# The first values of an attention layer: the two halves of the sum taken in turn over four token tiles, in four PSUM banks, with the loads in that order

## The chip, the cores and the metric

The kernel runs on one core of one Trainium2 chip. Its time is the device time in microseconds of one execution; a lower time is better. The core has five engines that run side by side, each with its own in-order queue: PE (matrix products; its weight loads, PEld, lie beside its products), DVE (vector), ACT (scalar, one function per element), POOL (general) and SP, which only issues DMAs here. DMAs are carried out by 16 DMA engines that the queues share.

## The reference, cut to what matters

The reference is a trunk of two layers: an attention layer and a recurrent layer, each followed by a SwiGLU feed-forward network, on one sequence of 1024 tokens of width 1024 in float32. The change touches only the start of the attention layer.

```
def reference(x, attn_w_in, ...):
    for layer in range(DEPTH):
        h = rmsnorm(x, norm_mix_pre[layer])
        if layer % 2 == 0:
            m = attention_mixer(h, attn_w_in[j], attn_rel_bias[j], attn_w_out[j])
...

def attention_mixer(h, w_in, rel_bias, w_out):
    proj = h @ w_in
    part_a, part_b = proj[..., :3 * A_W], proj[..., 3 * A_W:]
    qa, ka, va = [...]
    qs, ks, vs = [...]
    out_a = chunked_relpos_attention(qa, ka, va, rel_bias)
    out_b = stick_breaking_attention(qs, ks, vs)
    return jnp.concatenate([out_a, out_b], axis=-1) @ w_out
```

There are 16 heads of width 64. The values v of four heads are 256 columns of `h @ w_in`: for each token a sum over 1024 input columns.

## The kernel before, in words

**Tiles.** A token tile is 128 tokens (t = 0 to 7). The inner dimension, 1024, is cut into eight kt of 128. Each float32 operand is held as a high and a low part in the matmul's faster float32 type, and a product is three matmuls: high by high, high by low, low by high (lines 291 to 293 for the values, 166 to 168 for queries and keys). `split` (lines 140 to 159) makes the two parts of a weight tile: a cast on ACT (L155), then the rest on DVE (L156).

**The start.** The input comes in twice. `x_t` is the input with the inner dimension on the partitions: four column groups c of 256 tokens (two token tiles), each in two halves q of four kt; one load is 512 KB (`load_cols`, L464). `take(c)` multiplies these by the norm's gain `g0` and splits them into `hT`: on ACT (L495) and then DVE (L496), four kt for each of the two halves. `x` itself comes in rows, a token tile per load of 512 KB (`load_rows`, L459); it serves only the norm's scale: `squares(t)` sums the squares of a row on ACT (L501), and POOL (L503, L504) makes the reciprocal root `rsc` of it. The value weights of four heads come as two halves of the inner dimension (`w_v[grp, 0]` and `w_v[grp, 1]`, L137, 512 KB each), matching q.

**The values.** `v_tile(grp, w, vt, t2)` makes the unscaled values of the token tiles 2·t2 and 2·t2 + 1 in one PSUM bank, 256 columns each: 2 x 8 x 3 = 48 matmuls of 256 columns, the first token tile over all eight kt, then the second. Four calls, 192 matmuls, make the first group. `evacuate(vt, t2)` empties the bank: ACT multiplies with `rsc` while it copies (L305 and L306, 128 columns each, two token tiles). The banks come from a pool `proj` with two buffers, and the first projection of queries (L166 to L168, `psq`) takes its banks from the same pool: its first half of the tokens can start when token tiles 4 and 5 have been emptied, its second half when 6 and 7 have. `spread(half)` turns four `rsc` into a row `rsb` with DVE (L511), PE (a pair of matmuls, L513) and a copy by ACT (L514).

**The order.** The kernel's text gives the priorities: weights half 0, `take(0)`, weights half 1, `v_tile` 0, `take(1)`, `v_tile` 1, the squares of rows 0 and 1, `evacuate` 0, `take(2)`, `v_tile` 2 and so on. The framework then lays out each engine's own order from a simulated timeline (line 1257), so that an instruction whose inputs come late by that timeline is overtaken by others of its engine. SP issues the loads in this order: `g0`, weights half 0, columns (0,0) and (0,1), weights half 1, columns (1,0), (1,1), (2,0), (2,1), rows 0 and 1, columns (3,0), (3,1), rows 2 and 3; then the query and key weights and rows 4 to 7 in between. Ahead of the first product PE runs 32 transposes of an identity (L483), which read no input.

**Scores.** Behind the first projection the attention's scores take banks of a third PSUM pool, `pp`, tag `sc`, three buffers (L399, L400).

Of the kernel before, what the change touches and what calls it, by code (L numbers as in the profile page):

```python
# [8 lines left out]
F32 = mybir.dt.float32  # L9
F32R = mybir.dt.float32r  # L10
BF16 = mybir.dt.bfloat16
AF = mybir.ActivationFunctionType
ALU = mybir.AluOpType
PSUM = bass.MemoryType.PSUM

P = 128
S = 1024
D = 1024
KT = D // P
# [80 lines left out]
class Trunk:  # L100
# [164 lines left out]
    def attention(self, x_src, xT_src, w_v, w_qk, bias_t, o_dst, hT, pools, open_first):  # L265
        nc, tc = self.nc, self.tc
        with ExitStack() as ctx:
            ap = ctx.enter_context(tc.tile_pool(name="att", bufs=1, reuse_waits="tile"))
            pp = ctx.enter_context(tc.tile_pool(name="attp", bufs=1, space=PSUM, side="right", reuse_waits="tile"))
            prj = ExitStack()  # L270
            prp = prj.enter_context(tc.tile_pool(name="attproj", bufs=1, space=PSUM, reuse_waits="tile"))
# [6 lines left out]
            def v_weights(grp):  # L278
                return [self.split(w_v[grp, j], 4, 256) for j in range(2)]

            def v_tile(grp, w, vt, t2):
                ps = prp.tile([P, 512], F32, tag="proj", bufs=2, name=self.uid("psv"))
                for tt in range(2):
                    t = 2 * t2 + tt
                    hh, hl = hT.half[t // 4]
                    tok = slice((t % 4) * P, (t % 4) * P + P)
                    o = ps[:, tt * 256:(tt + 1) * 256]
                    for kt in range(KT):
                        wh, wl = w[kt // 4]
                        k4 = kt % 4  # L290
                        nc.tensor.matmul(o, hh[:, kt, tok], wh[:, k4, :], start=kt == 0, stop=False)
                        nc.tensor.matmul(o, hh[:, kt, tok], wl[:, k4, :], start=False, stop=False)
                        nc.tensor.matmul(o, hl[:, kt, tok], wh[:, k4, :], start=False, stop=kt == KT - 1)
                psvs[t2] = ps.rearrange("p (a h b) -> p a h b", a=2, h=2)

            psvs = {}

            def evacuate(vt, t2, both=False):
                psv = psvs.pop(t2)
                for tt in range(2):  # L300
                    t = 2 * t2 + tt
                    if both:
                        nc.vector.tensor_scalar(vt[0][:, t, :], psv[:, tt, 0, :], rsc[:, t:t + 1], None, op0=ALU.mult)
                    else:
                        nc.scalar.activation(vt[0][:, t, :], psv[:, tt, 0, :], AF.Copy, scale=rsc[:, t:t + 1])  # L305
                    nc.scalar.activation(vt[1][:, t, :], psv[:, tt, 1, :], AF.Copy, scale=rsc[:, t:t + 1])  # L306

            def steps(vt):
                for v in vt:
# [8 lines left out]
            def v_alloc():  # L318
                return [ap.tile([P, NT, P], F32, tag="v", bufs=3, name=self.uid("v")) for _ in range(2)]
# [133 lines left out]
            vt = v_alloc()  # L453
            small = ap.tile([P, 64], F32, name="small")
            ssc, rsc, g0 = small[:, 0:NT], small[:, 8:8 + NT], small[:, 16:16 + KT]

            def load_rows(t):
                x = ap.tile([P, D], F32, tag="st", bufs=12, name=self.uid("x0"))
                self.last_load = nc.sync.dma_start(x, x_src[t * P:(t + 1) * P, :]).ins  # L459
                return x  # L460

            def load_cols(c, q):
                x = ap.tile([P, D], F32, tag="st", bufs=12, name=self.uid("xt")).rearrange("p (k t) -> p k t", k=4)
                nc.sync.dma_start(x, xT_src[c, q])  # L464
                return x

            nc.sync.dma_start(g0, self.io["g0col"])
            grp = seq[0] // 2
            cols, rows_in = {}, {}
            raws = [self.raw(w_v[grp, 0], 4)]  # L470
            cols[0] = [load_cols(0, 0), load_cols(0, 1)]
            raws.append(self.raw(w_v[grp, 1], 4))
            for c in range(1, 4):
                cols[c] = [load_cols(c, 0), load_cols(c, 1)]
                if c > 1:
                    for t in (2 * c - 4, 2 * c - 3):
                        rows_in[t] = load_rows(t)

            ones = ap.tile([P, 640], F32, tag="nata", bufs=3, name=self.uid("ones"))[:, 0:P]
            nc.vector.memset(ones, 1.0)  # L480
# [2 lines left out]
                nc.tensor.transpose(warm[:, 0:P], self.ident, self.ident)  # L483
            rsb = ap.tile([P, S], F32, name="rsb")

            def take(c):
                hh, hl = hT.half[c // 2]
                ts = slice((c % 2) * 256, (c % 2) * 256 + 256)
                for q in range(2):
                    x = cols[c][q]  # L490
                    for k in range(4):
                        kt = 4 * q + k
                        g = g0[:, kt:kt + 1]
                        hi = hh[:, kt, ts]
                        nc.scalar.activation(hi, x[:, k], AF.Copy, scale=g)  # L495
                        nc.vector.scalar_tensor_tensor(hl[:, kt, ts], x[:, k], g, hi.bitcast(F32),  # L496
                                                       op0=ALU.mult, op1=ALU.subtract)

            def squares(t):
                x = rows_in[t]  # L500
                nc.scalar.activation(x, x, AF.Square, scale=D ** -0.5, accum_out=ssc[:, t:t + 1])  # L501
                r = rsc[:, t:t + 1]
                nc.gpsimd.tensor_scalar(r, ssc[:, t:t + 1], EPS, None, op0=ALU.add)  # L503
                nc.gpsimd.tensor_tensor(r, r, self.neghalf, op=ALU.pow)  # L504
# [8 lines left out]
                nc.tensor.matmul(ps, ones, d, start=True, stop=True)  # L513
                nc.scalar.copy(rsb[:, half * HALF:(half + 1) * HALF], ps)  # L514

            w0 = self.split(None, 4, 256, raw=raws[0])
            take(0)
            wv = [w0, self.split(None, 4, 256, raw=raws[1])]
            v_tile(grp, wv, vt, 0)
            take(1)  # L520
            v_tile(grp, wv, vt, 1)
            squares(0); squares(1)
            evacuate(vt, 0)
            take(2)
            v_tile(grp, wv, vt, 2)
            squares(2); squares(3)
            evacuate(vt, 1)
            take(3)
            v_tile(grp, wv, vt, 3)
# [8 lines left out]
            wq = self.split(None, KT, P, raw=wq)  # L538
            squares(4); squares(5)
            evacuate(vt, 2)  # L540
            squares(6); squares(7)
            evacuate(vt, 3)
# [4 lines left out]
            for j, p in enumerate(seq):  # L547
# [4 lines left out]
                if j < 7:  # L552
                    q = seq[j + 1]
                    if q % 2 == 0:
                        wv = v_weights(q // 2)
                        vt = v_alloc()
# [704 lines left out]
```

## Time and profile before

| What | us |
|---|---|
| Median of 3 runs | 2187.07 |
| The runs | 2186.4, 2187.07, 2189.74 |
| The profiled execution | 2190.47 |
| its span, first to last instruction | 2188.7 |
| PE's first product of the values (L291) | at 6.95 |
| PE's first projection product (L166) | at 35.62 |

The profile is of one execution. In its views a line of a timeline has the start, the duration, the engine, the line of the kernel, the operation, the tile written and the tiles read, and, where the engine stood idle ahead of it, for how long and what ended the idle time. The granted clock of PE is given as a share of full speed. A matmul's duration in the trace is longer than the distance to the next one, since matmuls overlap; what a matmul costs PE is that distance.

### The profile page before, as it was taken

To read this page: it belongs to the slowest core of one execution; us is meant where nothing else is said; L and a number is where in the kernel's file an instruction comes from. 1 tells how busy PE (TensorE), PEld (TensorE's weight loads), DVE (VectorE), ACT (ScalarE), POOL (GpSimd) and SP (SyncE) were. 2 spreads that over 40 slices of the span, in tenths; PEclk is the share of its full clock that TensorE was granted. 3 is DMA by queue.
4 is the path that set the end of the run, shared out by engine and by line. 5 is a ranking of instruction groups with operands and counts; after the bars stand their busy time and mean duration, and the time that the engine had idled before them with its cause. 6 is when DMAs were issued, how large, how long until landed. Compare 5 with 4: busy or idle time off the path is not lost.

```text
span 2188.7 us, 30464 instructions
## 1 busy us (share of the span) xinstructions
PE 2160.6 (99%) x11140; PEld 1803.1 (82%) x11140; DVE 1502.0 (69%) x2458; ACT 1171.6 (54%) x2174; POOL 210.3 (10%) x398
## 2 busy tenths in 40 slices
PE   9999999999999999999999999999999999999998
PEld 8898989878788888888887777888788888888886
DVE  4747555556877677767768678437786767758675
ACT  6656555556855545433446676538755454424453
POOL 2111113121100000000002333102100000000011
PEclk9999999999999999999999999999999999999999
DMA  7111011126334233336468411356233333328565
GB/s 284 44 40 59 30 38 56 45 93 216 135 98 138 92 121 96 112 100 242 135 194 241 128 57 39 110 189 228 76 131 101 122 96 102 106 87 292 169 182 155
DMA packets 169039, 272.32 MB, mean 124 GB/s; under 512 B 14140, under 2 KB 95036, under 8 KB 168888
## 3 DMA queue, kind: packets, MB, share of 16 engines
q1 hardware_dynamic: 168248, 268.27, 38.3%
q10 hardware_dynamic: 640, 2.10, 0.3%
q8 instruction: 87, 1.43, 0.3%
q14 instruction: 64, 0.52, 0.1%
HBM read 202.69 MB, written 65.54 MB: 123 GB/s over the span
## 4 chain that ended last, share of the span: by engine, by line
PE 88%; DVE 4%; DMA 3%; ACT 2%; issue 2%; POOL 0%; SPq 0%; POOLq 0%; ACTq 0%; DVEq 0%
PE ps L752 13%; PE ps L753 13%; PE ps L751 13%; PE ps L594 7%; PE ps L837 5%; PE ps L838 5%; PE ps L836 5%; PE pso L366 3%; PE tr L431 3%; PE psq L166 3%; PE psq L167 2%; PE psq L168 2%; PE ps L166 2%; PE ps L167 2%; PE ps L168 2%
## 5 line engine op out<-in xcount | busy, mean ns | idle before, releaser
L752 PE MATMUL ps<-hS,q 128*128 128x512 f32 (+1 forms) x1288 | 489.8, 380 | 0.5 <-DVE hS L89 0.5
L751 PE MATMUL ps<-hS,q 128*128 128x512 f32 (+1 forms) x1288 | 490.0, 381 | 0.0
L753 PE MATMUL ps<-hS,q 128*128 128x512 f32 (+1 forms) x1288 | 489.3, 380 | 0.0
L722 DVE TENSOR_TENSOR q<-raw,q 128x512 fp32r<-128x512 f32 x308 | 205.6, 687 | 175.1 <-ACT q L721 174.3
L752 PEld LDWEIGHTS ps<-hS,q 128*128 128x128 f32 x1288 | 242.9, 189 | 47.1 <-DVE hS L89 0.9
L751 PEld LDWEIGHTS ps<-hS,q 128*128 128x128 f32 x1288 | 242.5, 189 | 46.4 <-DVE tf L89 0.5
L753 PEld LDWEIGHTS ps<-hS,q 128*128 128x128 f32 x1288 | 243.0, 189 | 45.6
L721 ACT CAST q<-raw 128x512 fp32r<-128x512 f32 x308 | 178.7, 616 | 172.5 <-DVE raw L730 116.9
L837 PE MATMUL ps<-o,o 128*128 128x512 f32 x616 | 240.2, 390 | 0.6 <-DVE o L832 0.6
L838 PE MATMUL ps<-o,o 128*128 128x512 f32 x616 | 237.9, 390 | 0.3 <-DVE o L966 0.3
L836 PE MATMUL ps<-o,o 128*128 128x512 f32 x616 | 221.6, 391 | 3.5 <-ACT o L965 3.0
L709 ACT ACTIVATE raw<-raw,gcol 128x256 f32<-128x256 f32 x352 | 150.4, 498 | 131.2 <-DMA raw<-in_ffn_w_up_dram 73.2
L831 ACT CAST o<-raw 128x512 fp32r<-128x512 f32 x184 | 110.3, 620 | 161.7 <-PE ps L838 49.4
L182 POOL TENSOR_SCALAR rs<-ss 128x1 f32<-128x1 f32 x52 | 25.2, 484 | 1420.3 <-ACT junk L178 1355.8
L832 DVE TENSOR_TENSOR o<-raw,o 128x512 fp32r<-128x512 f32 x184 | 123.5, 689 | 54.4 <-ACT o L831 53.7
L836 PEld LDWEIGHTS ps<-o,o 128*128 128x128 f32 x616 | 115.4, 188 | 30.5 <-ACT o L965 5.1
L837 PEld LDWEIGHTS ps<-o,o 128*128 128x128 f32 x616 | 115.7, 188 | 25.8 <-DVE o L832 2.1
L838 PEld LDWEIGHTS ps<-o,o 128*128 128x128 f32 x616 | 115.6, 188 | 24.8 <-DVE o L966 1.2
L156 DVE TENSOR_TENSOR wlo<-raw,whi 128x1024 fp32r<-128x1024 f32 x76 | 93.6, 1231 | 57.4 <-ACT whi L155 56.3
L419 DVE TENSOR_TENSOR_SCAN pr<-pr,zero 128x128 f32<-128x128 f32 (+7 forms) x64 | 86.6, 1358 | 51.3 <-POOL pr L416 49.6
L155 ACT CAST whi<-raw 128x1024 fp32r<-128x1024 f32 x76 | 79.7, 1049 | 48.5 <-PE ps L167 19.9
L166 PE MATMUL psq<-hT,whi 128*128 128x512 f32 x256 | 102.3, 400 | 0.2 <-DVE st L337 0.2
(206 smaller groups left out, 4263.8 us busy)
## 6 DMA issues: line engine op xcount, KB each, us to landing
raw<-in_ffn_w_gate_dram SPq DMA_DIRECT2D x44, 512.0 KB, 4.2
raw<-in_ffn_w_up_dram SPq DMA_DIRECT2D x44, 512.0 KB, 4.2
gS<-c SPq DMA_DIRECT2D x88, 256.0 KB, 3.7
raw<-gS SPq DMA_DIRECT2D x88, 256.0 KB, 2.9
gA<-c SPq DMA_DIRECT2D x66, 256.0 KB, 3.3
raw<-in_ffn_w_down_dram SPq DMA_DIRECT2D x63, 256.0 KB, 4.4
raw<-gA SPq DMA_DIRECT2D x44, 256.0 KB, 2.8
t<-in_ffn_w_down_dram SPq DMA_DIRECT2D x22, 512.0 KB, 6.6
```

The source lines that it names most:

```text
L166: nc.tensor.matmul(ps, wh[:, kt, cols], hh[:, kt, :], start=kt == 0, stop=False)
L594: self.matmul = nc.tensor.matmul(ps[:, n * 512:(n + 1) * 512], x, y[:, n, :], start=first and i == 0, stop=last and i == len(passes) - 1).ins
L709: nc.scalar.activation(raw[:, i], raw[:, i], AF.Copy, scale=gain[:, 4 * k + i:4 * k + i + 1])
L721: self.last = nc.scalar.copy(t[:, 0], src).ins
L722: self.last_lo = nc.vector.tensor_tensor(t[:, 1], src, t[:, 0].bitcast(F32), op=ALU.subtract).ins
L751: nc.tensor.matmul(ps, a[:, 0, kt, :], bh, start=kt == 0, stop=False)
L752: nc.tensor.matmul(ps, a[:, 0, kt, :], bl, start=False, stop=False)
L753: self.matmul = nc.tensor.matmul(ps, a[:, 1, kt, :], bh, start=False, stop=kt == 3).ins
L832: tt(t[:, 1], src, t[:, 0].bitcast(F32), op=ALU.subtract)
L836: nc.tensor.matmul(ps, a[0], b[:, 0], start=first, stop=False)
L837: nc.tensor.matmul(ps, a[0], b[:, 1], start=False, stop=False)
L838: nc.tensor.matmul(ps, a[1], b[:, 0], start=False, stop=last)
```

## The change

The first four token tiles of the first value group are made together. For each half q of the inner dimension the weights' half is split, then for c = 0 and 1 the columns of (c, q) are taken and the twelve matmuls of this half are issued for the two token tiles of c. The four sums stay open meanwhile, in four banks: token tiles 0 and 2 in the two banks of `proj`, 1 and 3 in two of the three banks of `sc`. Token tiles 4 to 7 are made as before. `evacuate` and its dictionary go by token tile in place of pairs. The loads are put in the order of use: weights half 0, columns (0,0), (1,0), weights half 1, columns (0,1), (1,1), then rows 0 and 1, columns (2,0), (2,1), rows 2 and 3, columns (3,0), (3,1). The load of `g0` is issued by ACT in place of SP.

```diff
+            def v_part(o, w, t, kts):
+                hh, hl = hT.half[t // 4]
+                tok = slice((t % 4) * P, (t % 4) * P + P)
+                psvs[t] = o.rearrange("p (h b) -> p h b", h=2)
+                for kt in kts:
+                    wh, wl = w[kt // 4]
+                    k4 = kt % 4
+                    nc.tensor.matmul(o, hh[:, kt, tok], wh[:, k4, :], start=kt == 0, stop=False)
+                    nc.tensor.matmul(o, hh[:, kt, tok], wl[:, k4, :], start=False, stop=False)
+                    nc.tensor.matmul(o, hl[:, kt, tok], wh[:, k4, :], start=False, stop=kt == KT - 1)
+
+            def v_bank():
+                return prp.tile([P, 512], F32, tag="proj", bufs=2, name=self.uid("psv"))
+
             def v_tile(grp, w, vt, t2):
-                ps = prp.tile([P, 512], F32, tag="proj", bufs=2, name=self.uid("psv"))
+                ps = v_bank()
                 for tt in range(2):
...
+                    v_part(ps[:, tt * 256:(tt + 1) * 256], w, 2 * t2 + tt, range(KT))
...
-            nc.sync.dma_start(g0, self.io["g0col"])
+            nc.scalar.dma_start(g0, self.io["g0col"])
             grp = seq[0] // 2
-            cols, rows_in = {}, {}
-            raws = [self.raw(w_v[grp, 0], 4)]
-            cols[0] = [load_cols(0, 0), load_cols(0, 1)]
-            raws.append(self.raw(w_v[grp, 1], 4))
-            for c in range(1, 4):
-                cols[c] = [load_cols(c, 0), load_cols(c, 1)]
-                if c > 1:
-                    for t in (2 * c - 4, 2 * c - 3):
-                        rows_in[t] = load_rows(t)
+            cols, rows_in, raws = {}, {}, []
+            for q in range(2):
+                raws.append(self.raw(w_v[grp, q], 4))
+                for c in range(2):
+                    cols[c, q] = load_cols(c, q)
+            for c in range(2, 4):
+                for t in (2 * c - 4, 2 * c - 3):
+                    rows_in[t] = load_rows(t)
+                for q in range(2):
+                    cols[c, q] = load_cols(c, q)
...
-            def take(c):
+            def take(c, qs=(0, 1)):
...
-            w0 = self.split(None, 4, 256, raw=raws[0])
-            take(0)
-            wv = [w0, self.split(None, 4, 256, raw=raws[1])]
-            v_tile(grp, wv, vt, 0)
-            take(1)
-            v_tile(grp, wv, vt, 1)
+            wv = []
+            banks = [(pp.tile([P, 512], F32, tag="sc", bufs=3, name=self.uid("psv")) if t % 2 else v_bank())[:, 0:256]
+                     for t in range(4)]
+            for q in range(2):
+                wv.append(self.split(None, 4, 256, raw=raws[q]))
+                for c in range(2):
+                    take(c, (q,))
+                    for tt in range(2):
+                        v_part(banks[2 * c + tt], wv, 2 * c + tt, range(4 * q, 4 * q + 4))
             squares(0); squares(1)
             evacuate(vt, 0)
```

More of the change, by code (lines that the diff above doesn't have):

```diff
@@ L281, in v_tile @@
+            def v_bank():
+                return prp.tile([P, 512], F32, tag="proj", bufs=2, name=self.uid("psv"))
             def v_tile(grp, w, vt, t2):
-                ps = prp.tile([P, 512], F32, tag="proj", bufs=2, name=self.uid("psv"))
+                ps = v_bank()
                 for tt in range(2):
[L284 to L293, printed above, removed]
@@ L294, in v_tile @@
-                psvs[t2] = ps.rearrange("p (a h b) -> p a h b", a=2, h=2)
+                    v_part(ps[:, tt * 256:(tt + 1) * 256], w, 2 * t2 + tt, range(KT))
             psvs = {}
             def evacuate(vt, t2, both=False):
-                psv = psvs.pop(t2)
-                for tt in range(2):
-                    t = 2 * t2 + tt
+                for t in (2 * t2, 2 * t2 + 1):
+                    psv = psvs.pop(t)
                     if both:
-                        nc.vector.tensor_scalar(vt[0][:, t, :], psv[:, tt, 0, :], rsc[:, t:t + 1], None, op0=ALU.mult)
+                        nc.vector.tensor_scalar(vt[0][:, t, :], psv[:, 0, :], rsc[:, t:t + 1], None, op0=ALU.mult)
@@ L304, in evacuate @@
                     else:
-                        nc.scalar.activation(vt[0][:, t, :], psv[:, tt, 0, :], AF.Copy, scale=rsc[:, t:t + 1])
-                    nc.scalar.activation(vt[1][:, t, :], psv[:, tt, 1, :], AF.Copy, scale=rsc[:, t:t + 1])
+                        nc.scalar.activation(vt[0][:, t, :], psv[:, 0, :], AF.Copy, scale=rsc[:, t:t + 1])
+                    nc.scalar.activation(vt[1][:, t, :], psv[:, 1, :], AF.Copy, scale=rsc[:, t:t + 1])
             def steps(vt):
@@ L484, in attention @@
             rsb = ap.tile([P, S], F32, name="rsb")
-            def take(c):
+            def take(c, qs=(0, 1)):
                 hh, hl = hT.half[c // 2]
                 ts = slice((c % 2) * 256, (c % 2) * 256 + 256)
-                for q in range(2):
-                    x = cols[c][q]
+                for q in qs:
+                    x = cols[c, q]
                     for k in range(4):
```

## The prediction

> **What bounds the kernel now.** I read the page's shares first, then busy time by stretch for the start, then the timelines of PE and ACT there.
>
> ```profile
> span 2188.7 us, 30464 instructions
> PE 2160.6 (99%) x11140; PEld 1803.1 (82%) x11140; DVE 1502.0 (69%) x2458; ACT 1171.6 (54%) x2174; POOL 210.3 (10%) x398
> ```
>
> PE has 28 us of idle time in the span. Whatever the change wins must come out of the first 58 us; behind them PE has hardly any idle time for a long way (x counts instructions; of each engine the busy time in the stretch; then granted clock, DMA share, GB/s):
>
> ```profile
> core 0: us, PE busy (x) PEld busy (x) DVE busy (x) ACT busy (x) POOL busy (x), PEclk, DMA share, GB/s
> 6.90:9.37 2.47, 2.39 (x13) 1.75 (x12) 2.47 (x7) 2.47 (x7) 0.00 (x0) 1.00 1.04 421
> 9.37:11.94 2.57, 0.89 (x3) 0.48 (x3) 2.42 (x5) 2.57 (x6) 0.00 (x0) 1.00 1.02 406
> 11.94:15.56 3.62, 3.62 (x17) 3.62 (x18) 3.62 (x10) 3.62 (x10) 0.00 (x0) 0.53 1.03 412
> 15.56:29.01 13.45, 13.45 (x114) 13.45 (x113) 8.21 (x20) 13.45 (x32) 3.56 (x10) 1.00 1.03 404
> 4.90:29.40 24.50, 22.74 (x162) 21.33 (x161) 17.50 (x39) 24.05 (x54) 3.95 (x10) 0.93 1.03 409
> 58.00:440.00 382.00, 381.32 (x2874) 337.62 (x2873) 232.85 (x428) 221.68 (x449) 60.85 (x122) 1.00 0.14 46
> ```
>
> The reader is to see three limits that lie close together. PE loses 9.37 to 11.94 nearly whole, then runs 3.6 us at half clock. ACT is busy 24.05 of 24.50 us. The DMA engines are full, at 409 GB/s, so a load of 512 KB lands every 524288 B / 409 GB/s = 1.28 us, whatever the order. PE's timeline has the edges:
>
> ```profile
> 6.95 0.39 PE L291 MATMUL psv<-whi,hT 128*128 128x256 f32 x1
> 10.68 0.80 PE L291 MATMUL psv<-whi,hT 128*128 128x256 f32 x2 [1.31 <-ACT whi L155]
> 11.94 0.43 PE L292 MATMUL psv<-wlo,hT 128*128 128x256 f32 x1 [0.34 <-DVE wlo L156]
> 29.01 1.02 PE L513 MATMUL tr<-diag,ones 128*128 128x512 f32 x2
> 29.99 0.28 PE L292 MATMUL psv<-wlo,hT 128*128 128x256 f32 x1
> 35.62 0.40 PE L166 MATMUL psq<-hT,whi 128*128 128x512 f32 x1
> 41.09 1.02 PE L513 MATMUL tr<-diag,ones 128*128 128x512 f32 x2
> ```
>
> The values' 192 matmuls run from 6.95 to 35.62, and both waits are for the second weight tile. The clock by stretches of 3.41 us, laid on the grid on which it changes:
>
> ```profile
> 8.73:12.14 3.41, 1.72 (x9) 1.12 (x9) 3.26 (x7) 3.41 (x8) 0.00 (x0) 1.00 1.02 408
> 12.14:15.55 3.41, 3.41 (x17) 3.41 (x17) 3.41 (x10) 3.41 (x10) 0.00 (x0) 0.50 1.03 413
> 445.64:449.05 3.41, 1.72 (x12) 1.44 (x12) 3.29 (x14) 2.80 (x6) 0.67 (x1) 1.00 1.03 405
> 1199.94:1203.36 3.42, 2.06 (x10) 1.41 (x9) 3.42 (x5) 1.10 (x2) 0.00 (x0) 1.00 0.45 108
> 1203.36:1206.77 3.41, 3.41 (x16) 2.79 (x16) 2.28 (x3) 1.15 (x2) 1.60 (x2) 1.00 0.89 271
> 449.05:452.46 3.41, 3.41 (x12) 2.72 (x12) 1.88 (x9) 2.19 (x8) 2.03 (x4) 0.50 0.61 224
> 1548.10:1551.50 3.40, 3.40 (x19) 3.40 (x18) 2.14 (x4) 3.22 (x8) 0.79 (x2) 0.51 0.41 167
> ```
>
> A stretch with 3.41 - 1.72 = 1.69 us of idle PE is followed by one at 0.50; one with 3.42 - 2.06 = 1.36 us is not. A halved stretch full of matmuls costs 3.41 / 2 = 1.7 us, and this execution has three. The Trainium skill ("TensorE: Matmul & The Clock Gate", section "Why this matters for your kernels") asks for no PE idle gaps over about 3 us. This trace is stricter, at 1.69 us; by the page the half clock at 12.14 would not have come from the wait, and 1.7 us less would be to be had in the profiled execution.
>
> **The change part by part.** *The small load goes to ACT's queue.* SP's first weight load moves up by one issue:
>
> ```profile
> 0.72 0.40 SPq L467 DMA_DIRECT2D small<-in_g0col_dram  x1
> 1.18 0.42 SPq L137 DMA_DIRECT2D raw<-in_attn_w_v_dram  x1
> 2161.47 0.50 ACTq L258 DMA_DIRECT2D out_dram<-x  x1
> ```
>
> That is 1.18 - 0.72 = 0.46 us for every landing while the DMA engines are full. On ACT the issue costs about 0.50, before the first weights have landed, so it hides. If the DMA engines start no earlier, the 0.46 is lost; if ACT's issue delayed its first cast, up to 0.50 more. I take 0.46.
>
> *The order of the sum.* Its first half needs weight half 0 and two column loads (launch positions 1 to 3); the second half needs positions 4 to 6. A block of four kt and two token tiles holds PE for 24 x 13.45 / 114 = 2.83 us, and ACT makes the operands of two such blocks in this time:
>
> ```profile
> 5.04 1.05 ACT L155 CAST whi<-raw 128x1024 fp32r<-128x1024 f32 x1 [3.03 <-DMA raw<-in_attn_w_v_dram]
> 6.39 3.30 ACT L495 ACTIVATE hT<-xt,small 128x256 fp32r<-128x256 f32 x8 [0.30 <-DMA xt<-in_x_t_dram]
> ```
>
> that is 3.30 / 2 = 1.65 us for one. So PE has 5.7 us of work while ACT makes the next block (1.65) and casts the second weights (1.05): the wait at 9.37 goes, and with it the half clock behind it. PE alone then takes: start 6.95 - 0.46 = 6.49; the first 12 matmuls as now, still paced by the split, about 2.3 us (first stretch above); 180 x 0.118 = 21.2; the pair on L513 with what it displaces, 29.99 - 29.01 - 0.12 = 0.86. Sum 30.8 against 35.62: 4.8 us early. The later column loads stand behind row loads now, two positions (2.6 us) later for c=2 and c=3. c=3's second half moves from position 12 to 14, landing at about 5.0 + 13 x 1.28 - 0.46 = 21.2 us (the first weights' cast starts at 5.04); PE wants it behind 6.5 of 8 parts of its 192 matmuls, at about 26, and ACT needs 1.65 us. If ACT did the squares of four rows first, PE could wait about 1 us there. I take 0.
>
> *What is late next: a PSUM bank.* The first projection (L166) writes the bank of token tiles 4 and 5, which ACT has to empty first (L305, L306), with a scale from the square of row 5 (L501). ACT's timeline there:
>
> ```profile
> 28.34 1.05 ACT L155 CAST whi<-raw 128x1024 fp32r<-128x1024 f32 x1
> 30.07 0.59 ACT L514 COPY rsb<-tr 128x512 f32<-128x512 f32 x1 [0.68 <-PE tr L513]
> 31.07 1.07 ACT L501 ACTIVATE x<-x 128x1024 f32<-128x1024 f32 x1
> 33.48 0.36 ACT L306 ACTIVATE v<-psv,small 128x128 f32<-128x128 f32 x1
> 38.88 0.36 ACT L306 ACTIVATE v<-psv,small 128x128 f32<-128x128 f32 x1
> ```
>
> The bank is free at 33.84, 1.8 us before PE asks now, 3.0 us after PE would ask at 30.8. From the square's start to the free bank it is 33.84 - 31.07 = 2.77 us. ACT is full up to 28.34 + 1.05 = 29.39 and the change takes no work from it, so it is done with that list at 29.39 - 0.46 = 28.9. Row 5's load does not hold it:
>
> ```profile
> L459 SPq DMA_DIRECT2D x<-in_x_dram x1: 327/327/327, 17.9 to 17.9; - x1
> DMA to landing us min/median/max: 10.3/10.3/10.3
> ```
>
> (17.9 + 10.3 = 28.2, or 27.8 with 0.46 off.) Bounds: square 5 next on ACT: 28.9 + 2.8 = 31.7. Today's order, with the copy and token tile 4's two outputs ahead but without the 0.68 us of waiting: 31.07 - 0.68 - 0.46 + 2.77 = 32.7. If the L513 pair is laid behind all 192 matmuls, the copy starts 30.8 + (30.07 - 29.01) = 31.9, the square 1.0 later, the bank is free at 35.7. The framework lays out each engine's order from a timeline of its own (line 1257), so I can't read the order. I take 32.3, between the first two, as row 5 has landed but today's order is the nearest row. PE then sits idle 32.3 - 30.8 = 1.5 us, between the 1.36 that kept the clock and the 1.69 that halved it; I take it as kept. The first projection starts 35.62 - 32.3 = 3.3 us earlier; its first half takes 41.09 - 35.62 = 5.47 us. What follows is the other half (bank of tiles 6 and 7, free at 39.24 now; its scale also feeds the second L513 pair):
>
> ```profile
> 38.62 0.83 DVE L511 TENSOR_SCALAR diag<-ident,small 128x128 f32<-128x128 f32 x1 [2.00 <-POOL small L504]
> ```
>
> It is ready at 39.45 now. PE would want it at 41.09 - 3.3 = 37.8, so it must move by 1.65 us; ACT's squares of rows 6 and 7 follow the bank, which moves by 33.84 - 32.3 = 1.5, and I let these be equal.
>
> *Four banks instead of two, outputs by token tile.* The outputs keep their count and shape (16 of 128x128). PE changes bank every 12 matmuls. Today's attention does so more often:
>
> ```profile
> 102.25 0.40 PE L399 MATMUL sc<-st,st 128*128 128x512 f32 x1
> 102.72 0.28 PE L292 MATMUL psv<-wlo,hT 128*128 128x256 f32 x1
> ```
>
> A pair of another bank's 512-column matmuls there takes 102.72 - 102.25 = 0.47, about four times the 0.118 of a 256-column one: nothing is lost. I take 0. The two borrowed banks are next wanted by the scores, after 58 us.
>
> **Sum.** Against the profiled execution (2190.47 us, of which 2188.7 span): 3.3 us less, 2187.2, since from 58 to 440 PE is idle 0.7 of 382 us and passes it on; behind 440 I take it as passed on too, at nothing. That execution stands 3.4 us, two halved stretches, above the median 2187.07 of the runs (2186.4 to 2189.74). The idle time before 12.14 halves the clock only if a stretch of the grid holds nearly all of the 2.57 us from 9.37, about (3.41 - 2.57) / 3.41 = one placement in four, if the grid lies anywhere. The Trainium skill (the same page, "What's actually happening") calls the window free-running; one profile can't show that. I take it that the median run lacks this one. Its values then end at 33.9, its first projection half at 39.4, and the second L513 pair waits for 39.45, so only 39.45 - 37.8 = 1.65 us are won: 2187.07 - 1.65 = **2185.4 us**.
>
> **The rivals.** A: *no bank wait.* Square 5 goes first, row 7 is early too, and the runs do have the half clock: 41.09 - (30.8 + 5.47) = 4.8 us, 2182.3. For it: the rows of the first tiles come earlier. Against: ACT's 24.05 of 24.50 us.
>
> B: *the bank wait takes the place of the wait removed.* PE's queue is in order; from about 1.5 to 1.7 us of idle time on, the price doubles. With the bank free at 35.7, idle 4.9 us, the projection's first half takes 5.47 + 1.7 and ends at 42.9, 3.4 us behind the median run's 39.45: 2190.5, slower. It decides where the L513 pair is laid: behind the 192 matmuls, and copy and square 5 wait in ACT's queue. For it: program order has that pair behind them. Against: it ran before the last quarter's end today. A worse order of rows 6 and 7 as well would bring it past 0.2%.
>
> C: *it does not do what it says.* The framework already pulled two or three matmuls of another token tile into the wait at 10.68; a laid-out order that leaves the second weights late again gives about 0: 2187.1.
>
> D: *bank changes idle PE so often that the clock halves for the first half of the matmuls*: 96 x 0.118 = 11.3 us more, 2198.4. The rows at 102 us and the clock of 1.00 from 58 to 440 speak against it. The Trainium skill (the same page, "A second HAM failure mode: psum-queue depth-cycling") tells of such a kernel.
>
> **How the numbers follow.** Forecast 0.50, A 0.17, B 0.20 (half past the 0.2% bound, with row 7 late too), C 0.09, D 0.04. About 0.2%, 4.4 us, is what a measurement of this kernel can tell from no change. Faster by more: A, 0.17. Slower: 0.10 + 0.04, and 0.02 of the forecast for a later order laid out worse: 0.16. The rest, 0.67, is within. The range reaches from A with 0.5 us more to B: 2181.8 to 2190.5; that leaves out D and the worse half of B, and some of C's and A's spread.
>
> **What would show it.** Right: no idle PE between 9 and 12 us, clock 1.00 there, the first projection (L166) near 32.3 us with ACT's output of tile 5 (L306) ended just before, and the second L513 pair near 37.8. Wrong: PE waiting for the column loads of c=3 near 26; L166 before 31 (A) or after 34 with 0.50 behind it (B); the second weights' cast (L155) behind more than four blocks; all earlier by 3 us at 58 but not at 440.

## The result and the profile after

The changed kernel takes 2182.76 us (median of 17 runs, 2179.06 to 2186.45), the kernel before, beside it, 2186.95 us (17 runs, 2184.28 to 2189.74). The ratio is 0.9981, with a 95% interval of 0.9974 to 0.9987: 0.0013 to 0.0026 of 2187 us, so 2.8 to 5.7 us less, 4.2 us by the medians. The forecast was 2185.4 us, 1.65 us less; the range of 2181.8 to 2190.5 holds the result.

The profiled execution of the changed kernel took 2180.38 us. Its shares:

```profile
span 2178.6 us, 30466 instructions
PE 2154.3 (99%) x11140; PEld 1801.9 (83%) x11140; DVE 1500.7 (69%) x2458; ACT 1170.7 (54%) x2174; POOL 208.2 (10%) x398
```

The spans of the two profiles are 2188.7 - 2178.6 = 10.1 us apart, over twice what the medians are apart. One pair of profiles can't price this change: three profiles of the unchanged kernel have spans of 2188.7, 2183.7 and 2186.6 us (the last two are from the experiments). So the reading below is made at marks that stand in every trace, over several executions.

The start by stretches of the changed kernel (columns as in the prediction):

```profile
9.00:12.00 3.00, 3.00 (x27) 3.00 (x26) 2.85 (x7) 3.00 (x8) 0.00 (x0) 1.00 1.03 415
12.00:15.50 3.50, 3.50 (x32) 3.50 (x31) 2.69 (x8) 3.50 (x9) 0.91 (x3) 1.00 1.02 406
4.90:29.40 24.50, 24.50 (x194) 24.02 (x193) 17.96 (x40) 24.21 (x56) 3.97 (x10) 1.00 1.03 409
```

PE is busy without a gap where it waited 1.31 and then 0.34 us before, and its clock is 1.00 where it was 0.53. The 1.76 us of idle PE in 4.90 to 29.40 are gone, while ACT and the DMA engines work as they did. The timelines of PE and ACT around the first projection:

```profile
31.34 0.28 PE L290 MATMUL psv<-whi,hT 128*128 128x256 f32 x1
31.50 0.37 ACT L308 ACTIVATE v<-psv,small 128x128 f32<-128x128 f32 x1 [0.68 <-POOL small L508]
31.76 0.36 ACT L309 ACTIVATE v<-psv,small 128x128 f32<-128x128 f32 x1
32.17 0.50 PE L166 MATMUL psq<-hT,whi 128*128 128x512 f32 x1 [0.56 <-ACT v L309]
37.79 1.13 PE L517 MATMUL tr<-diag,ones 128*128 128x512 f32 x2
```

L290 is the last matmul of the values, L309 the output that frees the bank (L306 before), L517 the `spread` pair (L513 before). PE waits 0.56 us for that bank, with ACT's output ended at 31.76 + 0.36 = 32.12, and the second pair stands at 37.79, 3.30 us ahead of the 41.09 of the first profile of before.

From about 35 us on, the instructions of PE, ACT, DVE and POOL come in the same order as before. So a later mark tells what is left of the gain. One is the row of attention's last part where PE waits 1.18 us for ACT's `pt`; in the profile of before, and then of after:

```profile
443.12 1.09 PE L366 MATMUL pso<-pt,v 128*64 128x128 f32 x16 [1.18 <-ACT pt L437]
```

```profile
439.88 2.40 PE L369 MATMUL pso<-pt,v 128*64 128x128 f32 x40 [1.18 <-ACT pt L440]
```

That is 443.12 - 439.88 = 3.24 us: attention hands on what the start won.

### The profile page after: what moved, and what is told of

Read it like the earlier page. It is cut to its first block, busy times and chain, and to the rows that moved or that the text cites. A ratio compares the mean times of both kernels' runs of the same rounds, so it can differ in the third digit from the quotient of the medians.

```text
span 2178.6 us, 30466 instructions
## 1 busy us (share of the span) xinstructions
PE 2154.3 (99%) x11140; PEld 1801.9 (83%) x11140; DVE 1500.7 (69%) x2458; ACT 1170.7 (54%) x2174; POOL 208.2 (10%) x398
## 4 chain that ended last, share of the span: by engine, by line
PE 87%; DMA 4%; DVE 4%; ACT 3%; issue 2%; POOL 0%; SPq 0%; ACTq 0%; DVEq 0%; POOLq 0%
PE ps L759 13%; PE ps L760 13%; PE ps L758 13%; PE ps L601 8%; PE ps L843 4%; PE ps L845 4%; PE ps L844 4%; PE pso L369 3%; PE tr L434 3%; PE psq L166 3%; PE psq L167 3%; PE psq L168 2%; PE ps L166 2%; PE ps L167 2%; PE ps L168 2%
## 5 line engine op out<-in xcount | busy, mean ns | idle before, releaser
L182 POOL TENSOR_SCALAR rs<-ss 128x1 f32<-128x1 f32 x52 | 23.4, 449 | 1417.3 <-ACT junk L178 1353.8
L166 PE MATMUL psq<-hT,whi 128*128 128x512 f32 x256 | 102.5, 400 | 0.7 <-ACT v L309 0.6
```

The costliest lines, as they stand in the source:

```text
L166: nc.tensor.matmul(ps, wh[:, kt, cols], hh[:, kt, :], start=kt == 0, stop=False)
```

## The experiments

Two theories stood against each other at first. **By the forecast**, the start is all: the wait goes, a bank wait comes, and how much is won depends on whether the half clock behind the old wait belongs to the usual run. **By the rival**, part of the gain comes from elsewhere: fewer halved stretches later on, or the banks. `filler` and `after_fill` do extra work that no output uses (identity transposes).

### The kernel before again, the clock alone, the bank wait alone, the small load alone

`same` is the kernel before, unchanged.

> The kernel before, unchanged, profiled once more. It asks whether the half clock at 12 us, which the first profile shows, belongs to the typical execution. Theory F (the forecast's): the window grid lies anywhere, and only about one execution in four has it; this profile then most likely shows a granted clock of 1.00 from 12 to 16 us, the values' last matmul near 34 us in place of 35.6, and the second-half pair of the spread still at 39.5 or later. Theory H: the wait of 9.4 to 11.9 halves the clock in most executions; the profile shows about 0.5 over 3.4 us behind the wait, wherever the grid lies, and the values end at 35 to 36 us. Both expect a time within 0.1% of the kernel before.

Measured: 2185.84 us (11 runs) against 2186.67 (30 runs of before on this chip); ratio 1.0002 [0.9993, 1.0011]. Its stretches around the wait:

```profile
9.97:13.38 3.41, 2.22 (x14) 1.82 (x15) 3.24 (x7) 3.41 (x8) 0.00 (x0) 1.00 1.02 411
13.38:16.79 3.41, 3.41 (x31) 3.41 (x30) 3.41 (x10) 3.41 (x10) 0.00 (x0) 1.00 1.02 408
```

```profile
39.90 1.02 PE L513 MATMUL tr<-diag,ones 128*128 128x512 f32 x2
```

This execution kept its clock, and its second pair stands at 39.90 in place of 41.09. So the half clock is not in every execution, as the forecast had it, and costs about 1.2 us at this mark, not the full 1.7. How often it comes, one profile can't tell.

`filler` puts eight transposes into the wait of the kernel before, behind the twelfth value matmul:

```diff
+                        if fill is not None and tt == 0 and kt == 3:
+                            for i in range(8):
+                                with self.behind([m]):
+                                    m = nc.tensor.transpose(fill[:, 0:P], self.ident, self.ident).ins
+                            held = [m]
...
-            v_tile(grp, wv, vt, 0)
+            v_tile(grp, wv, vt, 0, turned_bank())
```

> The kernel before with eight identity transposes, which read no input, laid on PE between the twelfth matmul of the values and the thirteenth, inside the wait of 9.4 to 10.7 us. It leaves the wait for the second weights and takes only the idle time. It does more work than needed, and its output stays that of the reference. Theory F: the clock is mostly kept anyway, so the median moves by less than 0.7 us (0.03%). Theory H: the half clock is worth 1.7 us in most executions, and the median falls by 1.2 to 1.7 us (ratio near 0.9993). Both expect in the profile a granted clock of 1.00 from 7 to 35 us, the wait for the second weight's low part still ending near 11.9 us, and the values' last matmul near 34 us.

Measured: 2185.97 us (11 runs), ratio 0.9998 [0.999, 1.0007]. In its trace the wait for the weights stands, part of it filled, and the clock is kept:

```profile
6.90:9.37 2.47, 2.46 (x20) 2.22 (x19) 2.47 (x7) 2.47 (x8) 0.00 (x0) 1.00 1.01 413
9.37:11.94 2.57, 1.79 (x12) 1.15 (x10) 2.42 (x5) 2.57 (x6) 0.00 (x0) 1.00 1.02 411
11.94:15.50 3.56, 3.53 (x29) 3.53 (x30) 3.56 (x10) 3.56 (x10) 0.00 (x0) 1.00 1.04 417
```

```profile
9.24 1.04 PE L299 MATMUL tr<-ident 128*128 128x128 f32 x8
10.71 0.80 PE L293 MATMUL psv<-whi,hT 128*128 128x256 f32 x2 [0.44 <-ACT whi L155]
11.97 0.38 PE L294 MATMUL psv<-wlo,hT 128*128 128x256 f32 x1 [0.35 <-DVE wlo L156]
```

It is 0.7 us below the kernel before by the medians, inside the noise; the interval allows at most 0.0010 of 2187 us, 2.2 us. With the 1.2 us that `same` shows, the clock alone is not the 4 us. That the transposes hold the clock is not shown: the stretches on which the clock is decided follow each other every 3.413 us (12.14 to 449.05 in the first profile is 128 of them), and counted back from this trace's halved stretch at 1190.75 us their borders lie at 9.74 and 13.15, near the 9.97 and 13.38 at which `same` kept its clock with nothing in the wait.

`free_banks` is the changed kernel with the values of token tiles 4 to 7 in banks that nobody wants soon:

```diff
-            v_tile(grp, wv, vt, 2)
+            v_tile(grp, wv, vt, 2, pp.tile([P, 512], F32, tag="o", bufs=1, name=self.uid("psv")))
...
-            v_tile(grp, wv, vt, 3)
+            v_tile(grp, wv, vt, 3, pp.tile([P, 512], F32, tag="sc", bufs=3, name=self.uid("psv")))
```

> The changed kernel with token tiles 4 and 5 in the bank that attention's output takes later, and 6 and 7 in the third bank of the scores, so that the first projection needs no bank that the rows' squares hold back. If the bank wait is what is late next, as the forecast says, the 0.56 us of idle time ahead of the first projection product at 32.17 is gone (start at 31.5 to 31.7 us), and the key projection's first product comes 0.6 to 1.0 us earlier than in the changed kernel; the time falls by as much, under 0.05%, which the medians can hardly tell. Rival: the projection weights or the hidden low parts come no earlier than the bank, and PE waits at the same place for another releaser; nothing is won.

Measured: 2179.39 us (8 runs), ratio 0.9970 [0.9959, 0.9980], the best so far. The first projection no longer waits, and the late mark moves too:

```profile
31.13 0.40 PE L166 MATMUL psq<-hT,whi 128*128 128x512 f32 x1
438.60 2.40 PE L369 MATMUL pso<-pt,v 128*64 128x128 f32 x40 [1.18 <-ACT pt L440]
```

So the bank wait of the changed kernel is real. The late mark moves by 439.88 - 438.60 = 1.28 us, more than the 0.56 us of that wait, and not by the wait alone: in this kernel the second L517 pair also stands elsewhere, behind the whole query projection (at 42.04 us in place of 37.79).

`g0_on_sp` is the changed kernel with the small load back on SP:

```diff
-            nc.scalar.dma_start(g0, self.io["g0col"])
+            nc.sync.dma_start(g0, self.io["g0col"])
```

> The changed kernel with the small load back on SP's queue, ahead of the first weights. The forecast priced the move at 0.46 us for every landing while the DMA engines are full: the first weights' cast starts at 4.9 to 5.1 us in place of 4.42, the other landings 0.4 to 0.5 us later, and the first projection's first product, held by the bank of token tiles 4 and 5, 0.3 to 0.5 us later (32.5 to 32.7). Rival: PE's warm-up transposes and ACT's backlog swallow the shift, and the first projection starts where it did, at 32.2. Either way the median moves by less than can be told (0 to 0.5 us).

Measured: 2181.6 us (11 runs), ratio 0.998 [0.9971, 0.9989], not told apart from the change. ACT's timelines of the changed kernel and then of this one:

```profile
0.73 0.41 ACTq L470 DMA_DIRECT2D small<-in_g0col_dram  x1
1.17 1.28 ACT L155 ACT_TABLE_LOAD   x1 [1.17 <-PEq L1258]
4.42 1.05 ACT L155 CAST whi<-raw 128x1024 fp32r<-128x1024 f32 x1 [1.97 <-DMA raw<-in_attn_w_v_dram]
```

```profile
0.72 1.28 ACT L155 ACT_TABLE_LOAD   x1 [0.72 <-PEq L1258]
5.14 1.05 ACT L155 CAST whi<-raw 128x1024 fp32r<-128x1024 f32 x1 [3.14 <-DMA raw<-in_attn_w_v_dram]
```

On ACT the issue pushes the table load by 0.45 us, and that hides: the cast waits 1.97 us more for its weights. Over seven profiles with the load on ACT the cast starts at 4.42 to 4.93 (mean 4.67), over seven with it on SP at 5.01 to 5.14 (mean 5.09): 0.42 us.

### The bank layout

The traces now showed something far behind the start that the forecast had not looked at. The timeline at the turn from attention to its output projection, in `same`, and then in the changed kernel:

```profile
482.96 0.59 ACT L449 COPY ob<-pso 128x512 f32<-128x512 f32 x1 [0.54 <-PE pso L366]
483.60 0.50 PE L594 MATMUL ps<-whi,first 128*128 128x512 f32 x1 [0.69 <-ACT ob L449]
```

```profile
480.72 0.50 PE L601 MATMUL ps<-whi,first 128*128 128x512 f32 x1
480.83 0.59 ACT L452 COPY ob<-pso 128x512 f32<-128x512 f32 x1 [0.54 <-PE pso L369]
```

Before, the output projection's second sum (L594, L601 after) waits 0.69 us until ACT has copied attention's last output out of its bank; after, it starts 0.11 us before that copy. The addresses in the compiled programs say why. The banks of the pool `pp` are laid out in the order in which its tags are first used. Before, the attention's output (`o`) comes first and lies in bank 4, the scores in 5 to 7. In the changed kernel the values touch `sc` first: the scores lie in 4 to 6, the output in 7. The output projection's second sum takes banks 4 and 5. Two kernels try this both ways, one changing only the layout before, one undoing only the layout after.

`warm_in_sc`, the kernel before with its warm-up transposes in a bank of `sc`:

```diff
-            warm = turned_bank()
+            warm = pp.tile([P, 512], F32, tag="sc", bufs=3, name=self.uid("warm"))
```

> The kernel before, with the warm-up transposes written to a bank of the scores' pool instead of the transposes' pool; nothing else. All three profiles of kernels with the old start show PE idle for 0.7 us near 483 us, ahead of the output projection's second sum and released by ACT's copy of the attention output's last bank; all three of the changed kernel's family lack it. Theory L (bank layout): the changed kernel touches the scores' banks before the output's bank, so the output's bank lies last (7) in place of first (4), and the output projection's second sum, in banks 4 and 5, no longer follows the bank that is emptied last. This kernel makes the same layout without the change: the idle time near 483 us is gone, the values' stage is as before (last product near 34 us), and the output projection comes 0.7 us earlier. Rival: the idle time goes with the earlier start (another order against the DMAs); then it is still 0.7 us here.

`o_first`, the changed kernel with its four sums in banks such that `o` is touched first:

```diff
-            banks = [(pp.tile([P, 512], F32, tag="sc", bufs=3, name=self.uid("psv")) if t % 2 else v_bank())[:, 0:256]
-                     for t in range(4)]
+            def spare(tag, bufs):
+                return pp.tile([P, 512], F32, tag=tag, bufs=bufs, name=self.uid("psv"))
+
+            banks = [b[:, 0:256] for b in (v_bank(), spare("o", 1), v_bank(), spare("sc", 3))]
```

> The changed kernel with token tile 1 in the bank of attention's output and token tile 3 in one of the scores' banks, so that the output's bank is touched first and lies where it lay before. Theory L: the start stays as in the changed kernel (first projection near 32.2 us), and the idle time of 0.7 us ahead of the output projection's second sum near 481 us is back. Rival: it stays away, as in the changed kernel.

Measured, first in `warm_in_sc`, then in `o_first`:

```profile
485.66 0.50 PE L594 MATMUL ps<-whi,first 128*128 128x512 f32 x1
485.77 0.59 ACT L449 COPY ob<-pso 128x512 f32<-128x512 f32 x1 [0.54 <-PE pso L366]
```

```profile
482.77 0.59 ACT L452 COPY ob<-pso 128x512 f32<-128x512 f32 x1 [0.54 <-PE pso L369]
483.41 0.50 PE L603 MATMUL ps<-whi,first 128*128 128x512 f32 x1 [0.69 <-ACT ob L452]
```

The wait goes without the change and comes back with it: the layout makes it, and nothing else in the change does. Every profile with the layout of before has 0.68 or 0.69 us there (the three of before, `filler`, `o_first`, `loads_alone` below), and none with the other (the changed kernel and `free_banks`, two profiles each, `g0_on_sp`, `after_fill`, `sum_alone`, `warm_in_sc`). The one time of each (2192.18 and 2187.85 us, chip's before 2188.26) says nothing of 0.69 us: `warm_in_sc` had three halved stretches, `o_first` one.

`warm_in_sc` also shows the old wait once more, this time with the half clock, and its second pair:

```profile
9.10:12.52 3.42, 1.71 (x10) 1.11 (x10) 3.25 (x7) 3.42 (x8) 0.00 (x0) 1.00 1.03 416
12.52:15.93 3.41, 3.41 (x19) 3.41 (x18) 3.41 (x10) 3.41 (x10) 0.00 (x0) 0.50 1.02 408
```

```profile
41.08 1.02 PE L513 MATMUL tr<-diag,ones 128*128 128x512 f32 x2
```

### The two halves of the change

`sum_alone` has the new order of the sum and its four banks, but the loads and `g0` of before:

```diff
-            nc.scalar.dma_start(g0, self.io["g0col"])
+            nc.sync.dma_start(g0, self.io["g0col"])
...
+            raws = [self.raw(w_v[grp, 0], 4)]
+            cols[0, 0], cols[0, 1] = load_cols(0, 0), load_cols(0, 1)
+            raws.append(self.raw(w_v[grp, 1], 4))
+            for c in range(1, 4):
+                cols[c, 0], cols[c, 1] = load_cols(c, 0), load_cols(c, 1)
```

> The changed kernel with the loads in the old order and the small load back on SP's queue: the new order of the sum alone. The columns of c=1 land at positions 5 and 6 then, 2.6 us later than the changed kernel has their first half. By the forecast's way of reckoning PE has the first half of two token tiles, 2.3 + 1.4 us of work, to about 10.6 us, and then waits for the second weights' low part or c=1's first half until about 11.9: 1 to 1.5 us of idle time in place of 2.2 (1.65 by the trace), the clock kept, the values' end at 32.3 to 33, the key projection's first product 0.5 to 1.0 us behind the changed kernel's. Rival: the new order without the loads is worth nothing, the wait moves and stays 2.2 us; the values end near 34 us as in the undisturbed kernel before.

`loads_alone` has the new loads, but the sum and the two banks of before:

```diff
-            for q in range(2):
-                wv.append(self.split(None, 4, 256, raw=raws[q]))
...
+            w0 = self.split(None, 4, 256, raw=raws[0])
+            take(0)
+            wv = [w0, self.split(None, 4, 256, raw=raws[1])]
+            v_tile(grp, wv, vt, 0)
+            take(1)
+            v_tile(grp, wv, vt, 1)
```

> The kernel before with the new order of the loads and the small load on ACT's queue, the sum in the old order. The laid-out order pulls a third token tile's first half into the wait by itself, since c=1's first half is there. By the forecast's reckoning the wait shrinks to 0.5 to 1.3 us (PE has 24 matmuls for it, 2.8 us), the values end at 32 to 33 us, so the loads' order carries most of the gain and the new order of the sum the rest. The bank layout is the old one, so by theory L the 0.7 us near 482 us stay. Rival: without the new order of the sum the second weights still come too late for PE's queue, whose order is fixed; the values end near 34 us.

Measured: `sum_alone` 2184.17 us (10 runs, 2178.86 to 2190.38), ratio 0.9983 [0.9972, 0.9994]; `loads_alone` 2186.31 us (median of eight of its ten runs; the other two took 3623 and 5455 us and are no part of its ratio), ratio 0.999 [0.998, 1.0]. PE around the old wait, in `sum_alone` and then in `loads_alone`:

```profile
9.40:12.00 2.60, 2.26 (x16) 1.74 (x14) 2.43 (x5) 2.60 (x6) 0.00 (x0) 1.00 1.04 414
```

```profile
9.40:12.00 2.60, 1.97 (x12) 1.37 (x11) 2.43 (x5) 2.60 (x6) 0.00 (x0) 1.00 1.03 411
```

Each alone leaves 0.34 or 0.63 us of recorded idle time there; together they leave none. At the late mark `sum_alone` stands at 441.39 and `loads_alone` at 441.17, against 441.93 in `same`, which kept its clock as well: 0.54 and 0.76 us, while both together win 1.7 (below). That is 0.4 us more than the two added up, with one profile of each half; why they win more together is not shown, but the order of the sum can only use what the loads bring in time. That `sum_alone` has 4.1 us by its medians, as much as the change, is not in its trace of the start. Its interval reaches down to 1.3 us, and its one profile is of its slowest execution.

### Repeats, and the bank wait filled

Three kernels were run a second time, unchanged: the changed kernel, `free_banks` and the kernel before.

> The changed kernel once more, against the kernel before on the same chip. What the traces so far add up to: the start wins 1.5 to 2.0 us where the old wait didn't halve the clock (first products of the key projection's second half 55.7 before, 53.7 to 54.2 after), the bank layout 0.7 us near 483 us, together 2.2 to 2.7 us; the half clock at 12 us adds 1.5 us in those executions of the kernel before that have it (two of the three profiles with the old wait so far). So a median 2.2 to 4.2 us lower, ratio 0.9981 to 0.9990. If the ratio is below 0.9978 again, something else is won that the traces don't show.

> The changed kernel without the bank wait, against the changed kernel on the same chip. Its profile had the key projection 1.3 us earlier than the first profile of the changed kernel, and no half clock in the whole run. If only the wait is won, its median lies 1.0 to 2.0 us below the changed kernel's (the bank wait was 0.56, 1.35 and 1.49 us in the profiles that had it, and the second L513 pair moved behind the whole query projection wins some more). If the idle time of the bank wait also halved the clock in many executions (rival B's price), it lies 2.5 to 3.5 us below, as the medians of two different chips so far do.

> The kernel before, profiled once more. The profiles with the old wait that had a half clock behind it had their grid so that a stretch of 3.41 us ended between 11.9 and 12.8 us; the one that kept the clock had ends at 10.0 and 13.4. If that place decides, this profile has a half clock behind the wait when a stretch ends there, and none otherwise; over all places of the grid that is 0.85 of 3.41 us, one execution in four. A half clock with the grid elsewhere would say that it is more frequent than that.

`after_fill` is the changed kernel with four transposes in the bank wait, behind the last value matmul:

```diff
+            fill = pp.tile([P, 512], F32, tag="sc", bufs=3, name=self.uid("fill"))
+            held = self.matmul
+            for i in range(4):
+                with self.behind([held]):
+                    held = nc.tensor.transpose(fill[:, 0:P], self.ident, self.ident).ins
...
-            st = project(seq[0], (wq, wk))
+            st = project(seq[0], (wq, wk), [held])
```

> The changed kernel with four identity transposes, which read no input, on PE between the last matmul of the first values and the first projection: the bank wait stays and its idle time is shorter by about 0.5 us. It does more work than needed, and its output stays that of the reference. If the idle time of the bank wait halves the clock in many executions, the median falls by 0.5 to 1.5 us against the changed kernel; if not, it stays within 0.5 us, and the difference between the changed kernel and the one with free banks is the wait itself.

| Kernel | us, median (runs) | ratio to before, 95% |
|---|---|---|
| changed, again | 2182.42 (11) | 0.9982 [0.9973, 0.9991] |
| `free_banks`, again | 2179.40 (7) | 0.9971 [0.9960, 0.9981] |
| `after_fill` | 2181.04 (11) | 0.9978 [0.9969, 0.9987] |
| before, one time | 2188.41 | - |

The chip's runs of before have a median of 2186.43 us (23 runs). Change and `free_banks` repeat within 0.4 us, and `free_banks` has the lowest median both times. `after_fill` lies 1.4 us below the change, with intervals that overlap. PE's timeline of the changed kernel, again, then of `after_fill`:

```profile
32.65 0.50 PE L166 MATMUL psq<-hT,whi 128*128 128x512 f32 x1 [1.36 <-ACT v L309]
38.28 1.13 PE L517 MATMUL tr<-diag,ones 128*128 128x512 f32 x2
440.37 2.40 PE L369 MATMUL pso<-pt,v 128*64 128x128 f32 x40 [1.18 <-ACT pt L440]
```

```profile
30.72 0.60 PE L542 MATMUL fill<-ident 128*128 128x128 f32 x4
32.25 0.50 PE L166 MATMUL psq<-hT,whi 128*128 128x512 f32 x1 [0.93 <-ACT v L309]
```

The bank wait is 0.56 us in one profile of the change and 1.36 in the other, and neither has half clock behind it. Whether it halves the clock in some executions, which the fill would prevent, stays open: no profile shows it, and 1.4 us with overlapping intervals doesn't settle it.

The kernel before, again, has the half clock behind the old wait:

```profile
7.98:11.40 3.42, 2.08 (x12) 1.68 (x13) 3.27 (x8) 3.42 (x8) 0.00 (x0) 1.00 1.04 418
11.40:14.81 3.41, 3.22 (x15) 2.92 (x15) 3.41 (x9) 3.41 (x10) 0.00 (x0) 0.50 1.02 408
```

```profile
40.89 1.02 PE L513 MATMUL tr<-diag,ones 128*128 128x512 f32 x2
442.90 1.31 PE L366 MATMUL pso<-pt,v 128*64 128x128 f32 x20 [1.18 <-ACT pt L437]
```

## Why the prediction was right, and where it was wrong

The range holds the result, but the gain was forecast too small: 1.65 us lies below the measured interval of 2.8 to 5.7. The mechanism at the start came as forecast; a term that was chosen and one that was put at nothing are where it fell short.

**Right: the start.** The wait at 9.37 is gone and the clock is kept. The column loads of c = 3 cost nothing: PE is busy all of 4.90 to 29.40. "What is late next: a PSUM bank" came as written: L166 was put at 32.3 and came at 32.17 and 32.65, released by the output of token tile 5, after 0.56 and 1.36 us of idle PE where 1.5 was forecast. The second pair was put at 37.8 and came at 37.79 and 38.28. The small load was put at 0.46 us and measured 0.42, hidden on ACT as forecast. The values ended a little later than the 30.8 forecast (last matmul at 31.34 in the first profile, 31.00 in the second); the bank wait took that up. Part of this is the start term, put at 6.49: the first product came at 7.51 and 6.77. The 32 transposes ahead of it begin 0.21 us apart and go over to 0.11 us at 6.73 us in the first profile, at 4.39 in the second; the forecast had no term for them.

**Wrong: "I take it that the median run lacks this one."** The step gave the half clock one placement in four, from a need of nearly all of the 2.57 us inside one stretch. Four profiles hold the old wait as it was (before, `same`, `same_again`, `warm_in_sc`), and three have the half clock behind it. At the late mark these three stand at 443.12, 442.90 and 443.08 (mean 443.03), `same` at 441.93; the changed kernel (twice) and `o_first` at 439.88, 440.37 and 440.41 (mean 440.22). So the start wins 443.03 - 440.22 = 2.8 us where the half clock was, and 441.93 - 440.22 = 1.7 us where it wasn't. The 1.65 us of the forecast fits the case that it chose, but three of the four profiles show the other case. And the fit is partly luck. For the kept clock the forecast had the first projection at 33.9 us and the second pair waiting until 39.45; in `same` they come at 34.43 and 39.90, and the pair waits for nothing. In the changed kernel the later end of the values and the shorter bank wait cancel.

**Wrong: "Four banks instead of two ... I take 0."** The bank changes themselves cost nothing, as said. But which tag of the pool is used first sets the layout of the banks, and that takes away 0.69 us at 483 us. Rows of that wait were in the trace of before, and nothing in the forecast asked which banks come to lie where.

**The sum with both.** 2.8 + 0.69 = 3.5 us with the half clock, 1.7 + 0.69 = 2.4 without; three to one makes about 3.2 us. The medians give 4.2 [2.8 to 5.7] and, the second time, 4.0 [2.0 to 5.9] us. The missing 0.8 to 1.0 us is inside both intervals. Two things far behind the start could hold it.

One is a halved stretch that begins at 445 to 450 us, and by which the same matmuls fall back by 1.3 to 1.6 us against `same`. It is in six of the fourteen profiles: in five of the seven without the whole new start, in one of the seven with it (`o_first`). It goes with the place of the grid in all fourteen, counted back from each trace's halved stretches in steps of 3.413 us: it comes where a border lies 5.19 to 6.35 us behind the late mark, and stays away where the nearest borders lie at 3.77 to 4.94 and at 7.19 us or more. Of the four profiles with the old wait, the three with the half clock at 12 us have this one too. With three of four before and one of seven after, it is worth (0.75 - 0.14) x 1.5 = 0.9 us, an estimate from few profiles.

The other is a wait for a norm's scale on POOL (L182), behind the output projection. In the profile of before, and then of after:

```profile
1542.57 2.56 POOL L182 TENSOR_SCALAR rs<-ss 128x1 f32<-128x1 f32 x1 [3.90 <-ACT mg L178]
1547.02 1.09 PE L222 MATMUL pst<-ident,mg 128*128 128x128 f32 x8 [2.16 <-ACT mg L212]
```

```profile
1535.42 0.35 POOL L182 TENSOR_SCALAR rs<-ss 128x1 f32<-128x1 f32 x1 [3.90 <-ACT mg L178]
1538.59 1.09 PE L222 MATMUL pst<-ident,mg 128*128 128x128 f32 x8 [0.88 <-ACT mg L212]
```

In five profiles (before, `warm_in_sc`, `loads_alone`, `sum_alone`, `o_first`) this instruction takes 2.56 or 2.96 us at 550 to 577 or 1516 to 1543 us, in place of 0.35 to 0.68, and PE waits 0.70 to 2.84 us for what follows from it. It does so there in no profile of the changed kernel, `free_banks`, `g0_on_sp` or `after_fill`, but in none of `same`, `same_again` and `filler` either. What makes it long isn't shown. A halved stretch at 1187 to 1195 us comes and goes too, in five profiles, four of them without the whole new start. No run was made that changes any of these alone, so what the missing part is stays open.

**The rivals.** A, no bank wait, fell: the wait is there in both profiles of the change. The half clock that it counted on is in three of the four profiles. Its time, 2182.3, is near the result for this reason and for one that it did not have, the layout; and `free_banks`, which makes A's condition true, goes lower, to 2179.4. B had the right mechanism, but the bank is free at 32.12, not 35.7. C fell with the first row of the stretches. D fell: the changed kernel changes bank every 12 matmuls at a clock of 1.00.

**What the bank wait still costs.** Without it, and with the second pair moved behind the query projection, L166 starts at 31.13 and 30.68 and the late mark is at 438.60 and 438.18 (`free_banks`, twice): 440.22 - 438.39 = 1.8 us, and 3.0 us by the medians on the chip that ran both.

## What to carry to other kernels

When a wait at the start is taken away, ask which buffer is then freed late and give the new user another: here two spare banks brought 3.0 us by the medians beside the 4 of the change. A buffer that is borrowed from a pool can move where the pool's other buffers lie, so look also far from the edit for a wait that a shared bank makes. And price a wait that can halve the clock over several executions, since whether it does so is decided anew in each.

## What the runs showed of the hardware

- **How little idle time halves the clock.** Matmul records overlap (0.28 us long, 0.118 us apart), so the recorded busy time overstates the work. By the distance of 0.118 us per 256-column matmul, the stretch before the half clock held 12 x 0.118 = 1.4 us of matmuls in `same_again`, 42% of 3.41 us, and less in the two others (x9, x10); 14 x 0.118 = 1.65 us, 48%, kept it in `same`. By recorded idle time there is no such order: 3.42 - 2.08 = 1.34 us was followed by half clock, and the 1.36 us of the prediction's stretch from 1199.94 (ten matmuls of 512 columns, about 2.3 us at 0.23) was not. The Trainium skill ("TensorE: Matmul & The Clock Gate", section "What's actually happening") has the clock fall after at least one idle window of about 3.4 us. These runs are stricter, since 1.4 us of work in a window didn't hold it.
- **The grid lies anywhere.** The halved stretch behind the same wait began at 11.40, 12.14 and 12.52 us, and `same`'s borders lay at 9.97 and 13.38. The same section of the Trainium skill calls the window free-running, and these borders agree.
- **The first landing varies.** The first weights' cast started between 4.42 and 4.93 us with the small load on ACT: half a microsecond between executions, more than that edit is worth.
